# A hybrid attention and conv-FFN block: the first up-projection unit by token halves, pools moved in SBUF, two weight sums of the down-projection by DMA

## The chip, the cores and the metric

The kernel runs on one core of a Trainium2 chip. The metric is the device time of one execution in microseconds. Five engines are named as in the profile: PE (TensorE, with PEld for its weight loads), DVE (VectorE), ACT (ScalarE), POOL (GpSimd) and SP (SyncE, which here only issues DMAs).

## The reference

One residual block for 512 tokens of width 2048, in float32. The attention half has eight stick-breaking heads and eight latent-attention heads; it is not touched here. The rest is:

```python
mixed = concat(rmsnorm(o_sb), rmsnorm(o_mla))              # 512 x 2048
x = x + rmsnorm(mixed @ w_o, g_attn_post)
h = rmsnorm(x, g_ffn_pre)
u = causal_depthwise_conv(h @ w_up, conv_w, conv_b)        # w_up 2048 x 11264, width 3
gate, val = split(u, 2)                                    # 5632 columns each
y = (gelu(gate) * val) @ w_down                            # w_down 5632 x 2048
x = x + rmsnorm(y, g_ffn_post)
```

## The kernel before

**Arithmetic.** Each float32 operand is cut into a high part (a cast to a rounded type on ScalarE, `sc.copy`) and a low part (the difference, on VectorE). A product is three matmuls: high by high, high by low, low by high.

**Order of the work.** The program is straight-line. The framework gives each engine one list of instructions in order, which its planner makes at build time: it follows the program's order and pulls an instruction forward when, by its plan, its inputs and its page in SBUF are there. A tile of a pool takes a page that an older tile held and waits for that tile's last reader. Pools are stacked from the left or the right end of SBUF; a pool opened where another was closed waits page by page.

**The end of the out-projection** (lines 675 to 711 and 779 to 787). `w_o` is multiplied in column blocks; the last 512 columns go as two blocks of 256 (`sub`), each token tile of 128 rows at a time (`last_cols`). In the second block, each tile's rows are then complete: `residual(t)` (line 738) takes the row statistics (VectorE, then GpSimd for the power), adds x, squares on ScalarE, stores the new x by a DMA from GpSimd's queue, and scales the rows. `transposed(t)` (line 754) turns them by TensorE, multiplies by the gain in sixteen small ScalarE operations (line 763) and splits them into `act_hi` and `act_lo` (line 734). Order: columns of t, transposes of t - 1, residual of t.

**The up-projection** (lines 797 to 936). 22 units of 256 gate and 256 value columns. A unit is a 2 x 2 block product (inner halves of `w_up` by token halves and gate/value halves) done with seven products of half size in place of eight. The left operands of the seven are a11, a12, a7 (which takes the place of a21) and a22 in `act_hi`/`act_lo`, and the sums a5, a6, a3 in pages of their own; `transposed` makes them for t = 2 and 3. The weight side: four raw quarters of 1 MB are loaded per unit (buffers `wr`, 4), sums of them are formed in place by VectorE (`plus`, line 806), and each of the seven is cast and split (`w_parts`, lines 800 and 802; pages `wh` and `wl`, 3 each). Order p1, p5, p6, p7, p2, p3, p4. Weight parts are made two products ahead of their use (`queue`, line 1141). After a unit, the convolution and the gated product run in small steps between products (`later`), and the result goes to `g_dram`.

**The down-projection** (lines 939 to 1041). 20 of the 22 units in 5 chunks of 4, each chunk in two column halves `q`, each again a sevenfold product of 24 matmuls with 512 columns. At the start of a chunk (`q == 0`, product 1) `g_sides(ch)` loads the chunk's gated rows (`gr`, 2 MB) and makes all seven operand sides in the order g11, g22, g5, g6, g7, g12, g3. Each product is added to accumulators in SBUF (`add_to`, line 960; the first chunk copies on ScalarE). Before the first chunk `open_down` closes the pools of the up-projection and opens those of the down-projection. The last two units and the end of the block follow in `last_steps`.

## Time and profile before

| what | value |
|---|---|
| median of 3 runs (lowest, highest) | 2146.14 us (2144.24, 2147.12) |
| profiled execution: time, span | 2146.34 us, 2144.6 us |
| TensorE busy | 2037.9 us, 95% |
| VectorE busy | 1583.2 us, 74% |
| ScalarE busy | 944.1 us, 44% |
| GpSimd busy | 122.3 us, 6% |
| mean granted TensorE clock | 0.972 of full speed |

The page has the busy time by engine, the span in 40 slices, the DMA queues, the chain of work that ended last, and the costliest groups. Other views give the waits of an engine by what ended them, the instructions in order of time, and the busy time in chosen windows. A matmul's shown duration is longer than its distance to the next one, because matmuls are pipelined; rates are taken from windows with their counts. [...]

### The profile page before, as it was taken

Reading aid. Unit: us, or ns where it says so; the run is one execution under the profiler, and the core shown is the slowest. Engines: PE = TensorE matmul, PEld = TensorE weight load, DVE = VectorE, ACT = ScalarE, POOL = GpSimd, SP = SyncE. Lnnn points to the kernel's source line nnn. Section 1 sums busy time; section 2 is a strip of 40 time slices with the busy share of each in tenths; the row PEclk is TensorE's granted clock in tenths of the full one; section 3 lists DMA queues with packets and bytes.
Section 4 is the critical chain, followed back from the end, with each engine's and each line's share of the span. In section 5 each row is a group of like instructions: output and inputs, shape, how many; then the busy total and the mean of one; then the engine's idle time right before and its main releaser. Section 6 shows DMA issues by size and latency. Waiting matters only on the chain.

```text
span 2144.6 us, 30034 instructions
## 1 busy us (share of the span) xinstructions
PE 2037.9 (95%) x12784; PEld 1819.6 (85%) x12784; DVE 1583.2 (74%) x1491; ACT 944.1 (44%) x1124; POOL 122.3 (6%) x147
## 2 busy tenths in 40 slices
PE   8999999999999569999999999999997999999996
PEld 6788788877888569999999999999997778778785
DVE  7355355776233679989889889889889788999985
ACT  6243234455323854544444444444444543343332
POOL 0000001122021200000000000000000000000004
PEclk9999999999999779999999999999998999999998
DMA  8322322211422342342342432432434344324252
GB/s 273 98 71 77 98 76 63 76 33 60 143 93 79 118 150 96 110 156 90 126 140 89 139 127 89 155 111 96 155 105 147 128 138 138 118 79 160 96 175 99
DMA packets 179062, 245.16 MB, mean 114 GB/s; under 512 B 8176, under 2 KB 127088, under 8 KB 178928
## 3 DMA queue, kind: packets, MB, share of 16 engines
q1 hardware_dynamic: 174048, 227.04, 32.9%
q0 software_dynamic: 4448, 15.73, 1.8%
q8 instruction: 100, 1.64, 0.3%
q10 hardware_dynamic: 432, 0.47, 0.1%
q14 instruction: 34, 0.28, 0.0%
HBM read 223.29 MB, written 19.92 MB: 113 GB/s over the span
## 4 chain that ended last, share of the span: by engine, by line
PE 84%; DVE 8%; ACT 3%; DMA 2%; issue 1%; POOL 0%; DVEq 0%; ACTq 0%; POOLq 0%
PE ps L858 40%; PE ps L991 15%; PE ps L111 8%; PE ps L112 8%; PE ps L113 8%; PE ps L258 2%; DVE wr L806 1%; DVE wl L802 1%; DMA wr<-in_w_in_dram 1%; PE ps L234 1%; ACT wh L800 1%; DVE x L1094 1%; DVE t L438 1%; DVE wl L107 0%; ACT wh L105 0%
## 5 line engine op out<-in xcount | busy, mean ns | idle before, releaser
L800 ACT CAST wh<-wr 128x2048 fp32r<-128x2048 f32 x228 | 435.1, 1912 | 575.1 <-DVE wr L806 227.2
L802 DVE TENSOR_TENSOR wl<-wr,wh 128x2048 fp32r<-128x2048 f32 x228 | 519.1, 2288 | 111.5 <-ACT wh L800 111.1
L858 PE MATMUL ps<-act_hi,wh 128*128 128x256 f32 x1408 | 395.5, 281 | 15.0 <-ACT wh L800 15.0
L858 PE MATMUL ps<-act_hi,wl 128*128 128x256 f32 x1408 | 394.1, 280 | 1.5 <-DVE wl L802 1.5
L858 PE MATMUL ps<-act_lo,wh 128*128 128x256 f32 x1408 | 393.9, 280 | 0.0
L806 DVE TENSOR_TENSOR wr<-wr 128x2048 f32<-128x2048 f32 x128 | 292.6, 2286 | 1.3
L107 DVE TENSOR_TENSOR wl<-wr,wh 128x1024 fp32r<-128x1024 f32 (+2 forms) x105 | 128.1, 1220 | 210.4 <-ACT wh L105 210.3
L858 PEld LDWEIGHTS ps<-act_hi,wh 128*128 128x128 f32 x1408 | 265.5, 189 | 15.4 <-ACT wh L800 15.4
L858 PEld LDWEIGHTS ps<-act_hi,wl 128*128 128x128 f32 x1408 | 265.8, 189 | 1.8 <-DVE wl L802 1.8
L858 PEld LDWEIGHTS ps<-act_lo,wh 128*128 128x128 f32 x1408 | 264.5, 188 | 0.0
L105 ACT CAST wh<-wr 128x1024 fp32r<-128x1024 f32 (+2 forms) x105 | 108.0, 1028 | 234.3 <-PE ps L112 98.9
L111 PE MATMUL ps<-wh,act_hi 128*128 128x512 f32 (+1 forms) x448 | 163.9, 366 | 8.0 <-ACT act_hi L182 6.7
L112 PE MATMUL ps<-wl,act_hi 128*128 128x512 f32 (+1 forms) x448 | 163.3, 365 | 1.7 <-DVE wl L107 1.6
L113 PE MATMUL ps<-wh,act_lo 128*128 128x512 f32 (+1 forms) x448 | 162.9, 364 | 0.0
L111 PE MATMUL ps<-act_hi,wh 128*128 128x512 f32 x368 | 146.8, 399 | 0.0
L112 PE MATMUL ps<-act_lo,wh 128*128 128x512 f32 x368 | 145.7, 396 | 0.0
L113 PE MATMUL ps<-act_hi,wl 128*128 128x512 f32 x368 | 144.6, 393 | 0.0
L111 PEld LDWEIGHTS ps<-wh,act_hi 128*128 128x128 f32 x448 | 84.9, 190 | 22.6 <-ACT act_hi L182 6.7
L112 PEld LDWEIGHTS ps<-wl,act_hi 128*128 128x128 f32 x448 | 85.2, 190 | 16.9 <-DVE wl L107 2.4
L858 PE MATMUL ps<-a3h,wh 128*128 128x256 f32 x352 | 98.6, 280 | 0.0
L858 PE MATMUL ps<-a6h,wh 128*128 128x256 f32 x352 | 98.5, 280 | 0.0
L858 PE MATMUL ps<-a5h,wh 128*128 128x256 f32 x352 | 98.5, 280 | 0.0
(315 smaller groups left out, 4337.9 us busy)
## 6 DMA issues: line engine op xcount, KB each, us to landing
wr<-in_w_up_dram SPq DMA_DIRECT2D x88, 1024.0 KB, 5.4
wr<-in_w_down_dram SPq DMA_DIRECT2D x44, 1024.0 KB, 6.2
wr<-in_w_in_dram SPq DMA_DIRECT2D x59, 512.0 KB, 3.7
wr<-in_w_o_dram SPq DMA_DIRECT2D x32, 512.0 KB, 3.5
g_dram<-bg POOLq DMA_DIRECT2D x22, 512.0 KB, 5.2
gr<-g_dram SPq DMA_DIRECT2D x5, 2048.0 KB, 9.9
acc<-in_x_dram SPq DMA_DIRECT2D x16, 256.0 KB, 4.7
x<-in_x_dram SPq DMA_DIRECT2D x16, 256.0 KB, 5.4
```

Of the source, the lines that this page charges most:

```text
L105: sc.copy(hi, raw)
L107: ve.tensor_tensor(lo, raw, f(hi), ALU.subtract)
L111: te.matmul(ps, lh, rh, start=start, stop=False)
L112: te.matmul(ps, lh, rl, start=False, stop=False)
L113: te.matmul(ps, ll, rh, start=False, stop=stop)
L234: te.transpose(dst, a(b, j), ident)
L258: te.matmul(dst, q[:, b * P:(b + 1) * P], k[:, k0:S], start=i == 0, stop=False)
L800: sc.copy(hi, w)
L802: ve.tensor_tensor(lo, w, f(hi), ALU.subtract)
L806: ve.tensor_tensor(w, w, v, ALU.add)
L858: te.matmul(dst, l[:, k, ms], r[:, k, :], start=fresh and k == 0 and m == 0 and i == 0, stop=k == 7 and i == 2, skip_group_check=True)
L991: te.matmul(bs[t], l[:, k, ts_], r[:, k, :], start=fresh and k == 0 and i == 0, stop=k == FU - 1 and i == 2, skip_group_check=True)
```

## The change

1. The first up-projection unit is no longer a sevenfold product. Its gate part is done plainly, first for tokens 0 to 255 (needs only tiles 0 and 1 transposed), then, after the transposes of tiles 2 and 3, for tokens 256 to 511; its value part follows for all 512 tokens. Its gate weights are loaded and split before the last out-projection columns, into pages that later hold a5 and a6.
2. `transposed` runs two tiles behind the columns instead of one; the gain is one VectorE operation for 512 columns instead of four ScalarE operations; two of the four row scalings go to VectorE. The left sides a5, a6, a7, a3 are made in one go after the gate (`left_sides`). x rows and gains are loaded earlier, into fewer pages.
3. The pool of weight pages moves to the left end, where the later weight pool takes its place; the other pools move to the right. The down-projection's pages take the places of `act_hi`, `act_lo`, the a5, a6, a3 pages and small pages; nothing is closed in between.
4. In the down-projection the order is p1, p2, p5, p6, p7, p3, p4. The sums w12 + w22 and w11 + w21 are made by DMAs that add in flight (`accum_op`, issued by GpSimd), reading the quarters from HBM a second time; the other two stay on VectorE. The operand sides are made one by one: those of the next chunk each right after the product that used the old one in the second column half, those of the first chunk during and after the last up-projection unit, in halves of two units. Side 6 has pages of its own in the place of the unit's output pages.
5. Gated results are stored in two halves; the rows for the final residual come in four loads; some buffer counts and the DMA scratch size change.

The core of the diff (left out: unchanged helpers, page bookkeeping, the old bodies of functions that are replaced as a whole):

```diff
-    wp_stack, wp = stacked("wp", 4, "right")
+    wp_stack, wp = stacked("wp", 4)
...
-    at_stack, at = stacked("at")
+    at_stack, at = stacked("at", side="right")
...
-    cp_stack, cp = stacked("cp")
-    fp_stack, fp = stacked("fp")
+    cp_stack, cp = stacked("cp", side="right")
+    tp_stack, tp = stacked("tp", side="right")
+    fp_stack, fp = stacked("fp", side="right")
...
+    def load_x2(t):
+        for c in range(4):
+            x2[t, c] = fpage("x2", 8)
+            sy.dma_start(x2[t, c], x[t * P:(t + 1) * P, c * 512:(c + 1) * 512])
...
+            if c % 2:
+                ve.tensor_scalar_mul(y[t, c], x2[t, c], r2)
+            else:
+                sc.activation(y[t, c], x2[t, c], AF.Copy, scale=r2)
+        if t + 2 < NT:
+            load_x2(t + 2)
...
+            ve.tensor_tensor(raw[t, c].rearrange("p (k x) -> p k x", k=4), ps.rearrange("p (k x) -> p k x", k=4),
+                             g_rep[:, c, :, None].broadcast_to([P, 4, P]), ALU.mult)
+            split_into(((a11, a12), (a21, a22))[t // 2][c // 2], c, t, raw[t, c])
...
+    def left_sides():
+        a5, a6, a3 = ((cpage(n + "h"), cpage(n + "l")) for n in ("a5", "a6", "a3"))
+        for t in (2, 3):
+            for c in range(2):
+                x21, x22 = raw[t, c], raw[t, c + 2]
                 ve.tensor_tensor(x22, x21, x22, ALU.subtract)
-                split_into(a5, ks, th, x22)
+                split_into(a5, c, t, x22)
...
+    def gated(unit, m, bg, bv):
+        sc.activation(bg, bg, AF.Gelu_apprx_tanh)
+        ve.tensor_tensor(bg, bg, bv, ALU.mult)
+        po.dma_start(g_dram[unit, :, m, :], bg)
+    def early_w(kg):
+        raw_ = new_raw([P, 4, 256])
+        sy.dma_start(raw_, w_up[kg * 512:(kg + 1) * 512, 0:256].rearrange("(k p) c -> p k c", p=P))
+        both = cpage(("a5h", "a5l", "a6h", "a6l")[kg], (2, 4, 256))
+        hi, lo = both[:, 0], both[:, 1]
+        sc.copy(hi, raw_)
+        ve.tensor_tensor(lo, raw_, f(hi), ALU.subtract)
+        return hi, lo
...
+    def plain_part(banks, ws, kg, hs, first):
+        wh, wl = ws
+        for kk in range(4):
+            for m in range(2):
+                ms = slice(m * P, (m + 1) * P)
+                dst = banks[m][:, hs]
+                ah, al = act_hi[:, 4 * kg + kk, hs], act_lo[:, 4 * kg + kk, hs]
+                for i, (l, r) in enumerate(((wh, ah), (wh, al), (wl, ah))):
+                    te.matmul(dst, l[:, kk, ms], r, start=first and kg == 0 and kk == 0 and i == 0,
+                              stop=kg == 3 and kk == 3 and i == 2, skip_group_check=True)
+    load_x2(1)
     for sub in range(2):
         ws = [load_w(w_o, kg * 512, 4, 1536 + sub * 256, 256) for kg in range(4)]
+        if sub == 0:
+            ws_g = [early_w(kg) for kg in range(4)]
         for t in range(NT):
             last_cols(sub, ws, t)
             if sub == 1:
-                if t > 0:
-                    transposed(t - 1)
+                if t > 1:
+                    transposed(t - 2)
                 residual(t)
-    transposed(NT - 1)
+    bank_g = [bank(), bank()]
+    for kg in range(4):
+        plain_part(bank_g, ws_g[kg], kg, lo_half, True)
+        if kg == 1:
+            transposed(2)
+    ws_v = [load_w(w_up, kg * 512, 4, DFF, 256) for kg in range(4)]
+    transposed(3)
+    for kg in range(4):
+        plain_part(bank_g, ws_g[kg], kg, hi_half, False)
+    bank_v = [bank(), bank()]
+    for kg in range(4):
+        plain_part(bank_v, ws_v[kg], kg, slice(0, S), True)
+    pair_g, pair_v = (tp.tile([P, 2, S], F32, tag=n, name=n, bufs=1) for n in ("ug", "uv"))
+    for m in range(2):
+        conv(bank_g[m], m, pair_g[:, m])
+    a5, a6, a3 = left_sides()
+    def first_values(_):
+        for m in range(2):
+            conv(bank_v[m], NFF + m, pair_v[:, m])
+            gated(0, m, pair_g[:, m], pair_v[:, m])
     fp_stack.close()
-    vp_stack.close()
     wp_stack.close()
...
-    wq_stack, wq = stacked("wq", 1, "right")
-    tp_stack, tp = stacked("tp")
-    def w_parts(w):
-        n, cols = w.shape[1], w.shape[2]
-        hi = wq.tile([P, n, cols], R32, tag="wh", name="wh", bufs=3)
+    wq_stack, wq = stacked("wq")
...
         def p1():
-            w[11] = q(0, 0)
+            pair = w_pair(*shape)
+            w[11] = quarter(0, 0)
+            return w_parts(w[11], pair)
+        def p2():
+            w[21] = quarter(1, 0)
+            return w_parts(w[21])
+        def p5():
+            w[12] = quarter(0, 1)
+            plus(w[11], w[12])
+            if added:
+                added(w[12], 1, 1)
...
         def p6():
-            w[22] = q(1, 1)
-            return w_parts(plus(w[11], w[22]))
+            w[22] = quarter(1, 1)
+            parts = w_parts(plus(w[11], w[22]))
+            if added:
+                added(w[11], 1, 0)
+            return parts
         def p7():
-            return w_parts(plus(w[12], w[22]))
-        def p2():
-            w[21] = q(1, 0)
-            return w_parts(w[21])
+            return w_parts(w[12] if added else plus(w[12], w[22]))
         def p3():
             return w_parts(w[22])
         def p4():
-            return w_parts(plus(w[11], w[21]))
+            return w_parts(w[11] if added else plus(w[11], w[21]))
+        if added:
+            return p1, p2, p5, p6, p7, p3, p4
         return p1, p5, p6, p7, p2, p3, p4
...
         def half():
-            return tp.tile([P, 2, 256], F32, tag="u", name="u", bufs=3)
+            return v2(pg_v())
...
+            bg, bv = [pg_v() for _ in range(2)], z["bv"]
+            def last(m):
+                conv(ug[:, m], 2 * unit + m, bg[m])
+                gated(unit, m, bg[m], bv[m])
+            later.extend(lambda m=m: last(m) for m in range(2))
+        def then(use, *ns):
+            def both(w):
+                use(w)
+                if ns[0] == 6:
+                    open_down()
+                for n in ns:
+                    g_side(0, n)
+            return both
+        if unit == NFF // 2 - 1:
+            return zip(sevenfold(quarter, (8, 256)), (m1, m5, then(m6, 1), then(m7, 2), m2, then(m3, 5),
+                                            then(m4, 6, 7, 3, 4)))
+        return zip(sevenfold(quarter, (8, 256)), (m1, m5, m6, m7, m2, m3, m4))
...
+    def g_side(ch, n):
+        if n == 1:
+            gr = [cpage(tag, (2, 2, S), F32) for tag in ("a5h", "a5l")]
+            for i, t in enumerate(gr):
+                u0 = ch * FU + 2 * i
+                sy.dma_start(t, g_dram[u0:u0 + 2].rearrange("u p f s -> p u f s"))
+            d["gr"] = gr
+        def part(f_, h):
...
+        def added(w, kh, nh):
+            po.dma_start(w, rows(kh, nh), accum_op=ALU.add)
...
+        def use(n, w):
+            name = {1: "X", 2: "X", 5: "D", 3: "D", 7: "C", 4: "C", 6: "Y"}[n]
+            fresh = n in (1, 5, 7, 6)
+            if fresh:
+                z[name] = [bank(), bank()]
+            down_product(z[name], w, d["g"][n], fresh)
+            if q == 1 and ch + 1 < NST:
+                g_side(ch + 1, n)
...
     def stream():
-        for unit in range(NFF // 2):
+        yield (lambda: None), first_values
+        for unit in range(1, NFF // 2):
...
-    nc = bacc.Bacc("TRN2", target_bir_lowering=False, num_devices=1, dynamic_dma_scratch_size=1024)
+    nc = bacc.Bacc("TRN2", target_bir_lowering=False, num_devices=1, dynamic_dma_scratch_size=2048)
```

## Rows read from the trace of the kernel before

**Rows 1.** The page, part 1: busy us (share of the span) and instructions of each engine.

```profile
PE 2037.9 (95%) x12784; PEld 1819.6 (85%) x12784; DVE 1583.2 (74%) x1491; ACT 944.1 (44%) x1124; POOL 122.3 (6%) x147
```

**Rows 2.** Waits of TensorE, whole span: instruction, releaser, us in total, times, longest.

```profile
PE ps L759 <- ACT v L752: 24.0, 4, 13.4
...
PE ps L991 <- ACT g5h L964: 15.3, 4, 4.5
...
PE ps L858 <- ACT wh L800: 15.0, 1, 15.0
...
PE ps L991 <- ACT g11h L964: 12.7, 1, 12.7
```

**Rows 3.** Windows by stage: length, then PE, PEld, DVE, ACT, POOL busy, PEclk, DMA, GB/s.

```profile
640.00:680.00 40.00, 40.00 (x219) 34.34 (x218) 11.89 (x12) 12.54 (x21) 6.04 (x4) 1.00 0.26 87
...
700.00:772.00 72.00, 31.54 (x205) 29.28 (x203) 46.48 (x85) 57.83 (x153) 13.75 (x24) 0.68 0.41 140
...
814.00:1644.50 830.50, 830.50 (x7053) 830.45 (x7052) 718.50 (x526) 382.48 (x295) 11.27 (x21) 1.00 0.37 121
...
1644.50:1669.60 25.10, 9.35 (x31) 6.52 (x29) 23.24 (x22) 11.99 (x13) 0.53 (x1) 0.66 0.41 147
...
1836.50:1922.20 85.70, 81.23 (x336) 64.70 (x336) 79.21 (x62) 33.59 (x21) 0.00 (x0) 0.96 0.37 123
...
2083.00:2128.00 45.00, 44.88 (x193) 35.83 (x191) 25.60 (x33) 15.09 (x32) 19.72 (x15) 1.00 0.32 112
...
2128.00:2144.60 16.60, 0.00 (x0) 0.00 (x0) 9.42 (x14) 2.89 (x6) 5.59 (x5) 0.62 0.34 126
```

**Rows 4.** Timeline of ScalarE and TensorE: first evacuation of the last columns; eight transposes.

```profile
700.28 0.47 ACT L708 ACTIVATE y<-ps,rs 128x256 f32<-128x256 f32 x1 [2.91 <-PE ps L113]
...
708.90 1.97 PE L759 MATMUL ps<-ident,v 128*128 128x128 f32 x8 [4.12 <-ACT v L752]
```

**Rows 5.** Groups by line and form, VectorE: count, busy us and mean ns, idle before.

```profile
L107 DVE TENSOR_TENSOR wl<-wr,wh 128x1024 fp32r<-128x1024 f32 x95 | 119.1, 1254 | 207.3 <-ACT wh L105 207.2
...
L865 DVE SCALAR_TENSOR_TENSOR bg<-ug,gvc,bg 128x511 f32<-128x511 f32 x44 | 30.9, 745 | 0.0
...
L390 DVE TENSOR_SCALAR aT<-aT 128x512 f32<-128x512 f32 x4 | 1.7, 425 | 0.1
...
L734 DVE TENSOR_TENSOR a5l<-y,a5h 128x512 fp32r<-128x512 f32 x4 | 2.7, 684 | 0.0
...
L802 DVE TENSOR_TENSOR wl<-wr,wh 128x2048 fp32r<-128x2048 f32 x28 | 63.9, 2288 | 16.2 <-ACT wh L800 16.2
...
L965 DVE TENSOR_TENSOR g5l<-gr,g5h 128x1024 fp32r<-128x1024 f32 x5 | 6.1, 1217 | 0.0
```

**Rows 6.** Groups by line and form, ScalarE: weight casts and small gain copies.

```profile
L800 ACT CAST wh<-wr 128x2048 fp32r<-128x2048 f32 x228 | 435.1, 1912 | 575.1 <-DVE wr L806 227.2 <-PE ps L858 167.5 <-issue 108.1
...
L763 ACT ACTIVATE y<-ps,gv 128x128 f32<-128x128 f32 x32 | 10.0, 433 | 0.0
```

**Rows 7.** Timeline of VectorE, 690 to 790 us: first and thirteenth operation of a run.

```profile
759.84 0.69 DVE L734 TENSOR_TENSOR a5l<-y,a5h 128x512 fp32r<-128x512 f32 x1
...
767.06 0.68 DVE L734 TENSOR_TENSOR a6l<-v,a6h 128x512 fp32r<-128x512 f32 x1
```

**Rows 8.** Timeline of TensorE, 765 to 778 us: neighbouring matmuls of 256 columns.

```profile
773.08 0.41 PE L858 MATMUL ps<-act_hi,wh 128*128 128x256 f32 x1
...
773.29 0.41 PE L858 MATMUL ps<-act_lo,wh 128*128 128x256 f32 x1
```

**Rows 9.** DMA issues: queue, count, KB each, median us to landing.

```profile
wr<-in_w_down_dram SPq DMA_DIRECT2D x44, 1024.0 KB, 6.2
...
g_dram<-bg POOLq DMA_DIRECT2D x22, 512.0 KB, 5.2
...
gr<-g_dram SPq DMA_DIRECT2D x5, 2048.0 KB, 9.9
...
gl<-g_dram SPq DMA_DIRECT2D x2, 512.0 KB, 3.3
```

279 lines of the change are left out of this document (138 added, 141 removed).

## The prediction, before the change was run

> **What bounds the kernel now.** I read the page's totals first: TensorE is busy 95% of the span [rows 1]. So time can only come out of places where TensorE stands still or runs at its lower clock. Next the waits of TensorE, longest first [rows 2]: 24.0 us before transposes, 15.0 us before the first up-projection matmul, 12.7 us before the first down-projection matmul, 15.3 us in four waits for the operand g5. All lie in two places, which the stage windows show [rows 3]. From 700 to 772 us TensorE is busy 31.5 of 72 us at a mean granted clock of 0.68 of full speed. From 814 to 1644.5 it is busy all 830.5 us: 7053 matmuls, 0.1178 us each, 39.55 us for a unit of 336, so the up-projection proper has nothing to give. From 1644.5 to 1669.6 it is busy 9.4 of 25.1 us. A later chunk of the down-projection takes 85.7 us with VectorE busy 79.2 of them. The last stage, 2083 to 2128, gives the free rate of a 512-column matmul: 45.0 us for 193, 0.233 us.
>
> The profiled execution took 2146.34 us, its span 2144.6, 1.74 us around it; the median of the three runs is 2146.14. My sum is against 2146.34. About 0.2% (4.3 us) is what a measurement of this kernel can tell from no change.
>
> **Part A: the first unit by token halves.** Common point: the first tile of the last out-projection columns is evacuated at 700.28 us [rows 4]. What the change adds ahead of it are four gate-weight loads with their splits, beside matmuls, where from 640 to 680 us TensorE is never idle and VectorE is busy 11.9 of 40 [rows 3]; I cost them at nothing. Without that cover they would cost up to 4 x 1.25 us (line 107 of [rows 5]).
> Before: unit 1 starts at 814 us [rows 3].
> After, TensorE's work from 700.3 to unit 1: 144 matmuls of three token tiles x 0.1178 = 17.0; 64 transposes at 1.97/8 = 0.246 [rows 4] = 15.8; the plain unit has 192 gate matmuls of 256 columns x 0.1178 = 22.6 and 96 value matmuls of 512 x 0.233 = 22.4, together 45.0 (5.5 more than the 39.55 of the seven-product unit it replaces). Sum 77.8, so not before 778.
> After, VectorE's work from 702, by the groups of [rows 5]: for each token tile 4 residual adds at the 0.745 of line 865's like operation, 2 of the scalings that move from ScalarE at 0.425, 4 gain products (in place of sixteen small ScalarE copies, line 763 [rows 6]) and 4 low halves at 0.69, and for two evacuating operations of 256 columns with the tiny statistics another 2 x 0.69: 10.7, four tiles 42.8. Value weights 4 x 1.25 = 5.0. Gate convolution 4 x 0.745 = 3.0. The left operands, now in one piece after the gate, 32 operations at 0.60 (from the first to the thirteenth of such a run 7.2 us pass [rows 7]) = 19.3. First weight split of unit 1: 2.2. Sum 72.3, so not before 774 if it never idled. ScalarE, 57.8 of 72 us now [rows 3], sheds the 64 small copies, at most 27.7 us, and stops being the slowest there.
> The dependences add to this. Transposes of tile 3 are finished on VectorE at about 702 + 42.8 + 5.0 + 5 of idle in the statistics chains = 755. The upper gate half (11.3 us) has by then partly run at a lowered clock; I end it at 762. The left operands reuse the pages of the gate weights, so they start only then: 762 + 3.0 + 0.8 + 19.3 + 2.2 = 787.3; the value product, 22.4 us, ends at 784 and hides most of it. Unit 1 starts at about 788: gain 814 - 788 = 26 us. Bounds: 36 if everything fits (778). At the other end the plain unit runs half at the lower clock, where a 256-column matmul takes 0.21 us [rows 8], which adds about 10, and the first raw weight waits for pages that the left operands hold, which adds a load of 6.2 [rows 9] and a cast and a low half of 1.9 + 2.3 [rows 5, 6]: some 20 in all, unit 1 at 808, gain 6. Putting the weight pool low bears on that last point alone: the conversion pages of the new pool then lie over the old weight pages, and the diff doesn't show which raw buffer lies over which late page.
>
> **Part B: the down-projection.** TensorE's work after the up-projection is 1680 + 192 matmuls x 0.2332 = 436.5 us; it took 2128 - 1644.5 = 483.5 [rows 3]. So 47 us are lost, 32.8 of them named waits (12.7 + 15.3 [rows 2] and two smaller ones), the rest the low clock after them.
> Why they are there: the seven operand sides of a chunk are made in one piece at its start. The g22 pages are held by the last product of the old chunk, and g5 is made after g22. The change makes each side right after its last use in the second half of the old chunk, and puts product 4 last: six products (6 x 5.6 us) of lead. The four waits for g5 go. Late next would be a weight of the next group: its raw buffer is freed by the split of product 4, as now, three products (16.8 us) ahead of its use, and load, cast and low half take 6.2 + 4.2. The loads of the gated rows, now two of 1 MB, stand among the weight loads on SP's queue and would hold those up if their pages were not free; the pages are last read for side 4 of the old chunk, seven products earlier.
> VectorE for a chunk: 79.2 us [rows 3], minus 4 sums by DMA x 2.29 (the size of line 802 [rows 5]) = 9.2, plus about 1.5 because 11 side operations of 1.217 [rows 5] become 22 of 0.684: 71.5, under TensorE's 336 x 0.2332 = 78.4. VectorE stops being the slower one.
> First chunk: sides 1, 2 and 5 are made during the last unit. Behind it VectorE has the last convolutions (3.0), gate products (1.4), side 6 (2.5; its page lies over the unit's output pages, so it waits for the convolution) and weight operations for products 5 and 6 (9.1): about 17 us against three products (16.8 us) before side 6 is needed. I leave 5 us there, 1 us at each of 4 chunk ends, 2 us of clock: loss 11 instead of 47, gain 36. Bounds: 46 if nothing stalls, 20 if VectorE still sets half of the waits.
>
> **The accumulating DMA** is not in the trace. Below, 6.2 us, a plain load of 1 MB; 9.9 us, 2 MB in one transfer; above, 19.8, twice that, if the destination is read and written again as separate passes [rows 9]. GpSimd's queue issues it; a 512 KB store from there lands after 5.2 us, a load of that size from SP after 3.3 [rows 9]. I take 10. How late may it be? For product 7 the sum into w12 can start when product 1 starts, and its split (1.9 + 2.3 us) must end when product 6 ends: 4 x 5.6 - 4.2 = 18 us. Below that it costs nothing; each microsecond above costs one in each of 10 groups. 19.8 would cost 18 us. Queued behind it on GpSimd is only the other sum, needed two products later; but VectorE and ScalarE take their queues in order, so a late sum also holds the PSUM additions behind it.
> [...]
>
> Edits with one answer: pool sides, tags, fewer spare buffers for statistics and junk, x rows and gains loaded earlier, the gated pages stored in halves (two issues on an idle queue), the final x2 rows as four larger loads. Each lies beside matmuls; zero. The tail after the last matmul (16.6 us) is unchanged.
>
> **Sum.** 2146.34 - 26 - 36 = 2084.3.
>
> **Rivals.** (1) Part A stalls elsewhere: VectorE's queue and the lowered clock eat it. For it: VectorE and TensorE have nearly equal sums (72 and 78) with crossing dependences, and the clock in the same stretch is 0.68 now. Against: ScalarE sheds up to 27.7 us. Gain 6: 2146.3 - 6 - 36 = 2104.
> (2) VectorE remains the bound of the down-projection, or the sums come at the upper bound. Against: the margin is 7 us a chunk. Gain 20 or 36 - 18: 2146.3 - 26 - 19 = 2101.
> (3) The sums by DMA are late: slower. If one takes L us, the loss is 10 x (L - 18) us; the 62 us are gone at L = 24.2, and at L = 30 the time is 2084 + 120 = 2204. [...] Against: it would have to be 14 us above the value taken, and the stores from that queue, issued while VectorE was 87% busy [rows 3], land 1.9 us later than a load from SP [rows 9]; hence its low chance.
> [...]
> (4) The planner places the sides or the new unit where they were: only one part works, 2110 to 2120.
>
> **How the numbers follow.** Forecast 0.68 (2062 to 2100), rival 1 0.11, rival 2 0.08, rival 4 with less than 0.2% left 0.03 and otherwise 0.03, rival 3 0.07. Predicted 2084. Low end: both best bounds, 2146 - 36 - 46 = 2064, less 2 for the transposes' clock: 2062. High end: both worst, 2146 - 6 - 20 = 2120. Outside is about 0.12. Faster by over 0.2%: 0.90; within: 0.03; slower: 0.07.
>
> **What would show it.** In the waits of TensorE, the lines on transposes and on g5 gone or below 3 us each; the first matmul of the second unit at 778 to 808; a chunk of 336 matmuls in 79 to 80 us; VectorE some 72 us in it. The issue list shows 20 accumulating transfers of 1 MB from GpSimd with their landing time: over 18 us, and a wait of TensorE or VectorE at product 7 must appear. Wrong would be a new wait before the left operands of the second unit longer than 10 us, or a granted clock under 0.8 in the plain unit.

## The result and the profile after

The changed kernel takes 2087.59 us (median of 4 runs, 2084.47 to 2090.9) against 2145.19 for the kernel before in the same comparison; the ratio is 0.9731, with a 95% interval of 0.9714 to 0.9748. The forecast was 2084.3, with a range of 2062 to 2120.

The profiled execution took 2090.9 us, its span 2089.1. Engine totals of the changed kernel (beside [rows 1]), and the longest waits of TensorE (beside [rows 2]: engine, tile, line, waited for, total, times, longest):

```profile
PE 2028.6 (97%) x12736; PEld 1821.4 (87%) x12736; DVE 1537.8 (74%) x1570; ACT 924.4 (44%) x1114; POOL 162.6 (8%) x189
```

```profile
PE ps L836 <- ACT act_hi L748: 9.9, 2, 7.5
PE ps L111 <- ACT act_hi L182: 7.8, 1, 7.8
PE ps L133 <- DVE diag L132: 6.4, 3, 5.4
PE ps L1117 <- DVE wl L884: 4.6, 3, 3.0
PE ps L1117 <- DVE act_hi L1055: 3.6, 4, 1.0
PE ps L945 <- DVE wl L884: 3.2, 1, 3.2
PE ps L945 <- ACT wh L883: 2.7, 1, 2.7
```

The 24 us before the transposes, the 12.7 us at the first down-projection matmul and the four waits for an operand side are gone. New is 9.9 us in the plain unit (L836). Line 945 is the up-projection's product, 1117 the down-projection's; line 884 makes a weight's low half, line 1055 adds a product from PSUM, where TensorE leaves it, to its accumulator in SBUF.

Stage windows of the changed kernel (window, length, busy us and instruction count of TensorE, weight loads, VectorE, ScalarE, GpSimd, then granted clock as a share of full speed, DMA share, GB/s), beside [rows 3]; the row from 784.20 to 789.20 is the start of the second unit, the two from 1626.40 on are the start of the down-projection:

```profile
560.00:640.00 80.00, 80.00 (x354) 66.23 (x354) 25.50 (x24) 23.87 (x35) 13.08 (x9) 1.00 0.42 136
...
700.00:772.00 72.00, 61.89 (x429) 57.88 (x429) 62.98 (x115) 43.84 (x90) 14.60 (x23) 0.93 0.38 131
...
784.20:789.20 5.00, 4.97 (x23) 4.98 (x24) 4.96 (x3) 1.90 (x1) 0.00 (x0) 0.50 0.03 12
784.20:1605.00 820.80, 820.77 (x6874) 820.78 (x6875) 702.94 (x526) 373.84 (x305) 21.17 (x39) 1.00 0.36 118
860.00:900.00 40.00, 40.00 (x338) 40.00 (x337) 34.29 (x27) 18.26 (x15) 1.08 (x2) 1.00 0.37 119
...
1626.40:1642.40 16.00, 12.21 (x53) 9.23 (x51) 15.96 (x23) 10.90 (x17) 1.10 (x2) 1.00 0.72 188
1642.40:1646.40 4.00, 3.98 (x11) 3.12 (x11) 2.89 (x2) 1.68 (x1) 0.00 (x0) 0.57 1.02 421
...
1860.00:1940.00 80.00, 79.04 (x342) 63.73 (x341) 71.54 (x71) 34.14 (x29) 5.15 (x4) 1.00 0.71 188
```

From 700 to 772 us TensorE is busy 61.9 of 72 us at a clock of 0.93, where it was busy 31.5 at 0.68. A chunk's 336 matmuls take 79 to 80 us (the same matmul of three chunks starts at 1794.86, 1874.60 and 1953.70), where one took 85.7. VectorE is busy for about 71 of 80 us there. At the start of the down-projection TensorE is busy for 12.2 of 16 us, and then at a clock of 0.57 for 4.

The two spans, cut at the same events (first evacuation of the last out-projection columns; start of steady work on the second unit; end of the up-projection; last matmul; end):

| stretch | before, us | after, us | difference | forecast |
|---|---|---|---|---|
| to the first evacuation | 700.3 | 695.9 | -4.4 | 0 |
| to the second unit | 113.7 | 88.3 | -25.4 | -26 |
| 21 units of the up-projection | 830.4 | 842.2 | +11.8 | 0 |
| down-projection and last stage | 483.1 | 445.6 | -37.5 | -36 |
| tail | 17.1 | 17.1 | 0 | 0 |
| span | 2144.6 | 2089.1 | -55.5 | -62 |

The two terms of the sum came out as forecast. Two stretches that I had costed at nothing moved by -4.4 and +11.8 us, and they are the whole 7 us by which this execution is above the forecast. The experiments ask whether the two terms are right for the reasons given, and where the other two come from.

### The profile page after: what moved, and what is told of

Read it like the earlier page. It is cut to its first block, busy times and chain, and to the rows that moved or that the text cites. A ratio compares the mean times of both kernels' runs of the same rounds, so it can differ in the third digit from the quotient of the medians.

```text
span 2089.1 us, 30179 instructions
## 1 busy us (share of the span) xinstructions
PE 2028.6 (97%) x12736; PEld 1821.4 (87%) x12736; DVE 1537.8 (74%) x1570; ACT 924.4 (44%) x1114; POOL 162.6 (8%) x189
## 4 chain that ended last, share of the span: by engine, by line
PE 81%; DVE 10%; DMA 4%; ACT 3%; issue 2%; POOL 0%; DVEq 0%; ACTq 0%; SPq 0%; POOLq 0%
PE ps L945 38%; PE ps L1117 12%; PE ps L111 9%; PE ps L112 9%; PE ps L113 9%; PE ps L258 2%; DVE wl L884 2%; PE ps L836 2%; DMA wr<-in_w_in_dram 1%; PE ps L234 1%; DMA wr<-in_w_down_dram 1%; DVE wr L888 1%; ACT wh L883 1%; DMA a5l<-g_dram 1%; DVE t L438 1%
## 5 line engine op out<-in xcount | busy, mean ns | idle before, releaser
L883 ACT CAST wh<-wr 128x2048 fp32r<-128x2048 f32 x221 | 421.7, 1912 | 606.5 <-DVE wr L888 275.0
L884 DVE TENSOR_TENSOR wl<-wr,wh 128x2048 fp32r<-128x2048 f32 x221 | 505.4, 2288 | 152.0 <-ACT wh L883 151.9
L945 PE MATMUL ps<-act_hi,wl 128*128 128x256 f32 x1344 | 381.7, 284 | 3.2 <-DVE wl L884 3.2
L945 PE MATMUL ps<-act_hi,wh 128*128 128x256 f32 x1344 | 381.5, 284 | 2.7 <-ACT wh L883 2.7
L945 PE MATMUL ps<-act_lo,wh 128*128 128x256 f32 x1344 | 381.2, 284 | 0.0
L945 PEld LDWEIGHTS ps<-act_hi,wl 128*128 128x128 f32 x1344 | 258.8, 193 | 3.4 <-DVE wl L884 3.4
L888 DVE TENSOR_TENSOR wr<-wr 128x2048 f32<-128x2048 f32 x104 | 237.8, 2287 | 1.2
L113 PE MATMUL ps<-wh,act_lo 128*128 128x512 f32 (+1 forms) x512 | 186.3, 364 | 0.0
L113 PEld LDWEIGHTS ps<-wh,act_lo 128*128 128x128 f32 x512 | 97.1, 190 | 15.7 <-DVE act_lo L183 0.4
L1117 PE MATMUL ps<-wh,act_lo 128*128 128x512 f32 x320 | 100.3, 390 | 0.0
```

Source lines behind the costliest of these rows:

```text
L113: te.matmul(ps, ll, rh, start=False, stop=stop)
L883: sc.copy(hi, w)
L884: ve.tensor_tensor(lo, w, f(hi), ALU.subtract)
L888: ve.tensor_tensor(w, w, v, ALU.add)
L945: te.matmul(dst, l[:, k, ms], r[:, k, :], start=fresh and k == 0 and m == 0 and i == 0, stop=k == 7 and i == 2, skip_group_check=True)
L1117: te.matmul(bs[t], l[:, k, ts_], r[:, k, :], start=fresh and k == 0 and i == 0, stop=k == FU - 1 and i == 2, skip_group_check=True)
```

## Experiments: the two parts

**The first unit as seven products again.** Edit: the plain unit and its early weights are taken out, the stream starts at unit 0.

```
-        yield (lambda: None), first_values
-        for unit in range(1, NFF // 2):
+        for unit in range(NFF // 2):
```

> The changed kernel with the first up-projection unit as seven products again, all else of the change kept (transposes evacuated by one VectorE operation, rows loaded early, sides of the pools, down-projection). Theory: the unit by token halves is what covers the transposes and the left operands; without it unit 2 starts some 25 us later and the time is 2109 to 2114. Rival: the evacuation of the transposes on VectorE and the unloaded ScalarE brought half of it or more; then 2095 to 2103.

Measured: 2111.63 us (2110.32 to 2113.1), 24.0 above the changed kernel. The theory held. Its waits and the same window:

```profile
PE ps L925 <- ACT wh L863: 25.0, 2, 24.9
PE ps L775 <- ACT v L767: 15.0, 2, 7.7
```

```profile
700.00:772.00 72.00, 29.52 (x202) 28.06 (x201) 64.65 (x106) 38.55 (x74) 11.18 (x18) 0.72 0.39 133
```

TensorE is back at 29.5 of 72 us although VectorE evacuates the transposes and ScalarE is unloaded (38.6 us, 57.8 before). From the first evacuation to the second unit's steady work it takes 112.6 us, against 113.7 before: these edits gave about 1 us by themselves. What gave the 24 us is work for TensorE that needs only what is ready.

**The two weight sums on VectorE again.**

```
-            if added:
-                added(w[12], 1, 1)
...
-            return w_parts(w[12] if added else plus(w[12], w[22]))
+            return w_parts(plus(w[12], w[22]))
```

(and the same for the sum into w[11].)

> The changed kernel with the two weight sums of products 7 and 4 on VectorE again (order 1, 2, 5, 6, 7, 3, 4 and everything else kept). Theory: the sums by DMA are worth what VectorE is then over TensorE's time. VectorE for a chunk goes from 71.5 to 71.5 + 4 x 2.29 = 80.7 us against TensorE's 78.4 to 79, so a chunk of 336 matmuls takes about 81 us instead of 79.5 and the whole 2093 to 2103 us, with the changed kernel at 2087.6. Rival: most of the gain of the down-projection hangs on the sums; a chunk goes back to the 85.7 us of before and the time to about 2087.6 + 5 x 6 = 2118. Second rival: the margin lies elsewhere and nothing changes, 2085 to 2090.

Measured: 2095.64 us (2094.03 to 2099.6), +8. One window of it:

```profile
1860.00:1940.00 80.00, 77.05 (x333) 61.92 (x332) 77.61 (x71) 33.12 (x28) 0.00 (x0) 1.00 0.39 129
```

333 matmuls in 80 us make about 81 us a chunk (the same matmul of the next chunk starts 81.3 us later), with VectorE busy 78. The theory held, and the sums by DMA are worth 8 us of the 37.5.

**The sides in one piece at the chunk's start.**

```
-            if q == 1 and ch + 1 < NST:
-                g_side(ch + 1, n)
+            if n == 1 and q == 0 and ch > 0:
+                for m in ORDER:
+                    g_side(ch, m)
```

> The changed kernel with the seven operand sides of the next chunk made in one piece at that chunk's start, as the kernel before does, instead of one after each product of the old chunk's second half (the sums by DMA stay). Theory: the lead of six products removed the four waits for sides; without it they come back at the four chunk starts, 3.8 us each as in the kernel before, with some 1.2 us of others each: 2087.6 + 20 = about 2108, and the waits of TensorE show sides at four places. Rival: with VectorE no longer the slower engine it makes the sides in time wherever they stand in the program: below 2093.

Measured: 2082.54 us (2079.66 to 2086.8), ratio 0.9697 (0.968 to 0.9713): no slower, and if anything 5 us faster. The theory fell. No wait for a side came back; TensorE's two longest waits in the down-projection (the second was 3.6 us in the changed kernel):

```profile
PE ps L1117 <- DVE wl L884: 4.1, 2, 3.0
PE ps L1117 <- DVE act_hi L1055: 1.2, 2, 0.7
```

**Both undone at once.** The edits of the last two together.

> The changed kernel with both undone at once: the two sums on VectorE and the seven sides made in one piece at each chunk's start; the order of products with 4 last, the pages of the sides and the sides made in the last up-projection unit stay. Each alone cost 8 us or nothing. Theory: either suffices to keep VectorE ahead, and both undone bring the waits at four chunk starts back, 5 us each on top of the 8: 2087.6 + 8 + 20 = about 2115. Rival: the order of the products and the separate pages of the sides did it, since no side then waits for the last product of the old chunk but the one that is needed last; then no more than the sums alone, 2093 to 2099.

Measured: 2094.72 us (2094.42 to 2096.19), the same as with only the sums undone. So the rival held: the six products of lead were not what removed the waits, with the sums by DMA or without. What this kernel still has of part B is the new order and the first chunk's sides in the last up-projection unit. Product 4 was last before too, and every side had pages of its own. New in the order is that product 2 stands between 1 and 5, and that side 4 (g22 before), whose page the old chunk's last product holds, is made last and not second. The sums carry 8 us of the 37.5, and the distance between matmuls, which other starts of the operands changed (below), about 4.5. So the order and the first chunk's sides carry some 25 us. How they share them was not tried.

The trace of the kernel before shows why TensorE waited for g5. One chunk start:

```profile
1826.27 1.06 ACT L964 CAST g22h<-gr 128x1024 fp32r<-128x1024 f32 x1 [0.45 <-PE ps L991]
...
1833.37 1.22 DVE L974 TENSOR_TENSOR gr<-gr 128x1024 f32<-128x1024 f32 x1
...
1831.83 3.70 ACT L800 CAST wh<-wr 128x2048 fp32r<-128x2048 f32 x2 [4.50 <-DVE wr L806]
1835.43 1.04 ACT L964 CAST g5h<-gr 128x1024 fp32r<-128x1024 f32 x1
...
1836.53 0.80 PE L991 MATMUL ps<-wh,g5h 128*128 128x512 f32 x1 [4.46 <-ACT g5h L964]
```

Side g22 starts when the old chunk's last product releases its page (0.45 us of idle, ended by TensorE). The difference for g5 is formed in place on VectorE, after g22 is done there, and its cast stands behind two weight casts on ScalarE. Where side 4 is made last, g5 no longer stands behind it, whether the sides are made early or late. That fits the run above, but no run goes back to the old order alone.

## Experiments: how late a sum by DMA may be

The landing time was the value taken. From the changed kernel's list of DMA issues (KB each, median us from issue to landing):

```profile
wr<-in_w_down_dram SPq DMA_DIRECT2D x44, 1024.0 KB, 7.0
...
wr<-in_w_down_dram POOLq DMA_DIRECT2D x20, 1024.0 KB, 10.0
```

Then each sum was lengthened by repeating it:

```
-            po.dma_start(w, rows(kh, nh), accum_op=ALU.add)
+            for _ in range(2):
+                po.dma_start(w, rows(kh, nh), accum_op=ALU.add)
```

> The changed kernel with each accumulating transfer made twice, the second behind the first into the same tile (so its output isn't the reference's): a sum then takes 20 us instead of 10. Theory (the threshold of the prediction): the sum for product 7 has 18 us, so 2 us are lost in each of 10 groups: 2087.6 + 20 = about 2108. Rival: the sum for product 4, issued behind product 6's split, has less; in the trace of the changed kernel it is issued at 1726 us and its cast and low half are done at 1740.8, some 4 us ahead of its product, so the threshold is 14 us, 6 us are lost in each group, and the time is about 2148.

> The changed kernel with each accumulating transfer made three times, one behind the other into the same tile (so its output isn't the reference's): a sum then takes 30 us. Theory (10 x (L - 18) us): 2087.6 + 120 = about 2208. Rival (threshold of 14 us, by the sum for product 4): 2087.6 + 160 = about 2248. If the sums are hidden by more than either says, below 2150.

Measured: 2245.04 us with two (+157, 15.7 for each of ten groups) and 2404.19 with three (+317). Both theory (+20, +120) and rival (+60, +160) were far too low. To see which sum it is, only that for product 7 was repeated:

```
                 added(w[12], 1, 1)
+                added(w[12], 1, 1)
```

> The changed kernel with only the sum for product 7 made twice, the second behind the first into the same tile, 20 us instead of 10 (so its output isn't the reference's); the sum for product 4 once. Both twice cost 157 us where the threshold of 18 us gave 20. Theory: the sum for product 7 has its 18 to 20 us (in the trace of the changed kernel it is issued at 1747.15 us and its cast must start by 1767.3), and the loss came from the sum for product 4: 2088 to 2108. Rival: a late cast of product 7 holds back everything behind it on ScalarE and VectorE, the splits for the next group and with them its own next sum among them, so that the loss comes round in each group: about half of the 157, 2165.

Measured: 2138.41 us (2135.71 to 2139.58), +51, where the free time of 18 to 20 us allowed at most 20; the rival (2165) was too high. The rows show how it goes. First and last issue of these transfers in the four kernels, from the line's own view (changed kernel; one sum twice; both twice; both thrice):

```profile
L1134 POOL DMA_DIRECT2D wr<-in_w_down_dram x20: 1268/1286/1368, 1623.8 to 2003.3; - x20
```

```profile
L1135 POOL DMA_DIRECT2D wr<-in_w_down_dram x30: 1283/1294/1369, 1619.3 to 2050.1; - x30
```

```profile
L1135 POOL DMA_DIRECT2D wr<-in_w_down_dram x40: 1282/1293/1367, 1619.9 to 2159.4; - x40
```

```profile
L1135 POOL DMA_DIRECT2D wr<-in_w_down_dram x60: 1275/1286/1371, 1621.0 to 2320.4; - x60
```

Ten groups stretch over 379.5, 430.8, 539.5 and 699.3 us: ten transfers more cost 51, the next ten 109, the next twenty 160. That is 5.1, 10.9 and 8.0 us for each transfer that is added to a group. So the transfers of a group are paid one after the other, those of the one sum and those of the other. GpSimd's and ScalarE's timelines of the kernel with one sum twice show a group (start, duration, then what ended the idle time before):

```profile
1709.99 1.28 POOL L1135 DMA_DIRECT2D wr<-in_w_down_dram  x1 [20.63 <-DVE act_lo L1086]
1720.26 1.29 POOL L1135 DMA_DIRECT2D wr<-in_w_down_dram  x1 [8.99 <-DMA wr<-in_w_down_dram]
1734.47 1.28 POOL L1135 DMA_DIRECT2D wr<-in_w_down_dram  x1 [12.92 <-issue]
1754.66 1.29 POOL L1135 DMA_DIRECT2D wr<-in_w_down_dram  x1 [18.91 <-DVE act_hi L1056]
```

```profile
1734.26 1.90 ACT L883 CAST wh<-wr 128x2048 fp32r<-128x2048 f32 x1 [12.33 <-DMA wr<-in_w_down_dram]
...
1743.38 1.92 ACT L883 CAST wh<-wr 128x2048 fp32r<-128x2048 f32 x1 [3.34 <-DMA wr<-in_w_down_dram]
```

ScalarE stands 12.3 us at the cast that waits for the sum of product 7; the sum for product 4 leaves GpSimd only at 1734.47, when that cast has begun; its own cast holds ScalarE again; and the next group's first sum leaves at 1754.66, 20 us behind. The casts of the next group's weights stand behind both. So the time to compare with TensorE's group (39 to 40 us) is not one sum's lead but the way round: both sums one behind the other and some 12 to 15 us of casts, low halves and VectorE additions. With 20 and 10 us a group takes 5.1 us more than the changed kernel's 39.5, which is 30 + 14.6; with 20 and 20 it takes 16.0 more, 40 + 15.5; with 30 and 30 32.0 more, 60 + 11.5. With 10 and 10 it would be 32 to 36: the changed kernel has 4 to 8 us in hand for both sums together, an estimate from these rows. What held the second sum until then the profile doesn't name ("issue"). The program makes it wait only for its loads and for the low half of product 6, which VectorE ended at 1727.4, 7 us earlier. But it leaves 0.3 us after the transfer ahead of it on GpSimd's queue has landed (1734.16), and in six of the ten groups of this run the profile names nothing for that wait (53.6 us of "issue" in all). In the changed kernel the second sum leaves 0.32 to 0.34 us after that landing in four of the ten groups, and none of its 20 sums leaves before the one ahead has landed. So these sums did not overlap here; why is open.

## Experiments: where operands start

**What costs 12 us in the up-projection.** Nothing in it waits (820.77 of 820.80 us busy), yet 40 us hold 338 matmuls (row 860 to 900 above) where they held 342. The first 5 us of it are at a clock of 0.50, behind the wait before the second unit: 24 matmuls start where 42 would, which makes about 2 of the 12. For the rest: in the trace the distance from one matmul to the next is 0.1200 us for products on act_hi and act_lo and 0.1178 for those on a5, a6 and a3; before it is 0.1178 for all. In the out-projection the reverse: 354 matmuls in 80 us (row 560 to 640 above), 349 before. The same two windows of the kernel before:

```profile
560.00:640.00 80.00, 80.00 (x349) 64.63 (x348) 24.64 (x23) 22.44 (x34) 13.12 (x9) 1.00 0.39 135
860.00:900.00 40.00, 40.00 (x342) 40.00 (x341) 34.66 (x27) 18.56 (x16) 0.53 (x1) 1.00 0.36 119
```

Two kernels of little but matmuls measured this by itself.

> Not the computation of the reference: only matmuls on float32r operands whose places in SBUF are set by hand, 96 of 256 columns (or 48 of 512) for each pair of places, first with the other engines nearly idle, then with VectorE, ScalarE or a load into SBUF working beside them near to and far from the operands. It is to tell why the spacing of 256-column matmuls in the changed kernel is 0.1200 us where weights and moving operand both lie low in SBUF and 0.1178 where they lie apart. Theory: the place alone decides, so the quiet stages show two levels, about 0.120 where both operands lie close together at one end and 0.118 where they lie apart. Rival: accesses of other engines collide with TensorE's reads; then all quiet stages are alike, and only the stages with traffic near the operands are longer, by some 0.002 us a matmul.

Stages of 256 columns and of 512 columns with the other engines nearly idle, then 256 columns beside VectorE, ScalarE and loads:

```profile
40.00:240.00 200.00, 200.00 (x1669) 200.00 (x1668) 11.92 (x18) 0.00 (x0) 0.00 (x0) 1.00 0.00 1
290.00:490.00 200.00, 200.00 (x884) 165.61 (x883) 24.90 (x36) 0.00 (x0) 0.00 (x0) 1.00 0.00 1
500.00:570.00 70.00, 70.00 (x586) 70.00 (x585) 50.49 (x27) 7.31 (x4) 0.00 (x0) 1.00 0.00 1
572.00:640.00 68.00, 68.00 (x569) 68.00 (x568) 4.30 (x7) 36.52 (x20) 0.00 (x0) 1.00 0.08 23
642.00:710.00 68.00, 68.00 (x569) 68.00 (x569) 4.71 (x11) 0.00 (x0) 0.00 (x0) 1.00 0.90 325
```

Both theories fell: 0.1200 us (0.2267 for 512 columns) at every place, and with all the traffic tried, near or far, a load at 325 GB/s among it: from copy to copy 96 matmuls take 11.47 to 11.58 us in every stage of 256 columns, 11.52 in most, beside VectorE, ScalarE and loads alike. All operands here start at the same offset modulo 256 bytes, which the kernels' do not, and that gave the next kernel:

> Not the computation of the reference: matmuls on float32r operands only, with nothing beside them, 48 of 256 columns (then 24 of 512) for each of 59 pairs of starting bytes of the weights and of the moving operand, counted past a multiple of 512. The run on places showed one spacing for every place and for traffic of any kind: 0.1200 us for 256 columns, 0.2267 for 512, all with both operands on the same multiple of 128 bytes. In the two kernels a pair with 0.1200 (or 0.2267) has both operands at the same offset modulo 128 bytes, a pair with 0.1178 (or 0.2333) at offsets that differ by 64. Theory: the offset of the one operand against the other modulo 128 decides; a pair (0, 64) or (64, 0) gives 0.1178 and 0.2333, a pair (64, 64) 0.1200 and 0.2267. Rival: the start of the moving operand alone decides, then (0, 64) and (64, 64) are alike; or the start has no effect and all pairs are at 0.1200, so that something else of the kernels makes it.

A matmul here has two operands: the weights, 128x128, each behind a weight load (12736 loads and 12736 matmuls in the changed kernel), and the moving operand of 256 or 512 columns (in the out- and down-projection the weights of a matmul are the activations' side). Of 59 pairs of starting bytes those with both at multiples of 64 bytes fall into four cases by their difference (moving minus weights, modulo 256; distance between matmuls in us):

| difference | 256 columns | 512 columns |
|---|---|---|
| 0 | 0.1200 | 0.2267 |
| 64 | 0.1178 | 0.2289 |
| 128 | 0.1187 | 0.2333 |
| 192 | 0.1133 | 0.2333 |

Each stage of 48 matmuls ends with a copy by VectorE, so the distance between two copies is the length of a stage. The stages with weights at 64 and the moving operand at 0, 64, 128 and 192 end at 109.06, 120.48, 131.80 and 137.50:

```profile
103.61 0.69 DVE L80 COPY res<-ps 128x512 f32<-128x512 f32 x1 [4.98 <-PE ps L78]
109.06 0.69 DVE L80 COPY res<-ps 128x512 f32<-128x512 f32 x1 [4.75 <-PE ps L78]
114.73 0.69 DVE L80 COPY res<-ps 128x512 f32<-128x512 f32 x1 [4.98 <-PE ps L78]
120.48 0.69 DVE L80 COPY res<-ps 128x512 f32<-128x512 f32 x1 [5.06 <-PE ps L78]
126.14 0.69 DVE L80 COPY res<-ps 128x512 f32<-128x512 f32 x1 [4.97 <-PE ps L78]
131.80 0.69 DVE L80 COPY res<-ps 128x512 f32<-128x512 f32 x1 [4.96 <-PE ps L78]
137.50 0.69 DVE L80 COPY res<-ps 128x512 f32<-128x512 f32 x1 [5.00 <-PE ps L78]
```

They take 5.45 us (difference 192), 5.75 (0), 5.66 (64) and 5.70 (128). The stages up to 58 us, with weights at 0 and 256 columns, are about 2% shorter at each difference (5.64 us at 0, 5.53 at 64, 5.59 at 128, 5.33 at 192) and are not in the table; no run shows why.

The theory held in its kind (the difference decides), with four levels modulo 256 instead of two modulo 128. It is not the difference alone: pairs off the multiples of 64 lie between 0.1133 and 0.1233 us (48 matmuls in 5.44 to 5.92 us). The operands of both kernels start 32 bytes past a multiple of 64. (The starts are those of the built programs; no trace has them.) Four pairs of this kind were measured: a difference of 0 gave 0.1200 and 0.2267 us, 64 gave 0.1178 and 0.2289, 192 gave 0.1178 and 0.2333. So for these operands the table holds but for 192 with 256 columns, which in these two kernels only short stages have.

In the kernel before, the up-projection is all at a difference of 64 (0.1178), the out- and down-projection at 192 (0.2333). In the changed one act_hi and act_lo against the weights are at 0 (0.1200), a5, a6 and a3 at 64 (0.1178); the out-projection is at 0 (0.2267), the down-projection at 192 for five sides (0.2333) and at 0 for the two in act_lo (0.2267). These are the distances found in the two traces. 4032 of the 7056 matmuls of the 21 units by 0.0022 us make 9 of the 11.8 us lost, and the low clock behind the wait the other 2.

**The kernel with other starts.** Only padding: 224 bytes fewer of small buffers below the operands, 32 bytes at the top, 64 ahead of the weight pool, so that the up-projection is at 192 throughout and the down-projection at 64. The 32 bytes bring the operands to multiples of 64; without them the difference of 192 would have given 0.1178 by the pairs measured.

```
+    po.memset(pad.tile([P, 8], F32, name="pad"), 0.0)
...
+    po.memset(wq.tile([P, 16], F32, name="wpad"), 0.0)
```

> The changed kernel with nothing but the starting bytes of its operands moved: 224 bytes fewer below the operands on the left side, 32 bytes at the top of the right side, 64 bytes ahead of the up- and down-projection's weights, so that in the up-projection every moving operand starts 64 bytes before its weights modulo 256, both at multiples of 64. By the run on starting bytes a 256-column matmul then takes 0.1133 us in place of 0.1200 (four of seven products) and 0.1178 (three of seven), and the down-projection's 512-column matmuls 0.2289 in place of 0.2333 (five of seven) and 0.2267 (two). Theory: the spacing carries over to the kernel: a unit of 336 takes 38.1 us instead of 40.0, 21 units 800 instead of 842, the down-projection some 4 us less; 2087.6 - 42 - 4 = about 2042. Rival: VectorE and ScalarE, 34 us of a unit, with their queue order become late and eat half: about 2065. Second rival: the spacing in the kernel has another cause and nothing changes: 2085 to 2090.

Measured: 2053.83 us (2049.49 to 2079.03), ratio 0.9563 (0.9547 to 0.9579): 34 us faster than the changed kernel, between theory and rival. One of the five executions, the profiled one, took 2079.03, the others, of which there is no trace, 2049.5 to 2054.5. In it 8 us hold 73 matmuls at first; behind one wait, at 793 us, 40 us hold 342 to the end of the up-projection, which is 0.1178 again:

```profile
784.00:792.00 8.00, 8.00 (x73) 8.00 (x72) 5.99 (x4) 3.65 (x4) 0.00 (x0) 1.00 0.00 0
800.00:840.00 40.00, 40.00 (x342) 40.00 (x341) 33.03 (x25) 18.27 (x15) 0.54 (x1) 1.00 0.30 95
```

So in one execution the spacing of 0.1133 was lost at a wait, where 0.64 us pass from one matmul to the next. The last kernel below waits at the same matmul, which there starts 0.43 us after the one before it, and keeps 0.1133. What switches it stays open.

## Experiments: a version that beats both

The changed kernel waits before its second unit. VectorE's timeline there:

```profile
768.88 0.69 DVE L749 TENSOR_TENSOR act_lo<-v,act_hi 128x512 fp32r<-128x512 f32 x1
778.03 1.43 DVE L810 SCALAR_TENSOR_TENSOR uv<-ps,gvc,uv 128x511 f32<-128x511 f32 x2 [8.46 <-ACT uv L809]
...
781.89 2.28 DVE L884 TENSOR_TENSOR wl<-wr,wh 128x2048 fp32r<-128x2048 f32 x1
```

The left operands end at 769.6; the next instruction in the queue is the value convolution, which needs the end of the value product; the weight split stands behind it, and TensorE waits for the split.

```
+        cast, low = made[2]
+        with tc.issue_after(cast), tc.issue_after(low):
```

> The changed kernel with the value convolution and gated product of the first unit queued on ScalarE and VectorE behind the weight splits of the second unit's first three products, instead of ahead of them. Theory: VectorE stands idle from 769.6 to 778.0 us because its next instruction waits for the end of the value product, and the first weight split stands behind it; with the split in that gap the second unit starts at about 778 instead of 784, which gives 5 to 6 us: 2082. Rival: the split waits anyway, since the pages of the new weights lie over those of the value weights, which the value product reads to its end; then at most 2 us: 2086.

Measured: 2080.89 us (2079.05 to 2081.29), 6.7 below the changed kernel. The theory held: the low half is made at 768.35 and the second unit starts at 773.5 us without a wait. That the raw weight's page, and not the queue, held it is refuted.

All three (this one behind the fourth split, the starts, the sides at the chunk's start):

> The changed kernel with three edits together: the starting bytes of the operands as in e7_starts (alone 2053.8 us, against 2087.6), the first unit's value convolution and gated product queued behind the weight splits of the second unit's first four products (behind three it alone gave 2080.9), and the sides made at each chunk's start (alone 2082.5). Theory: the first two add up, the third gives 0 to 5 us: 2053.8 - 6.7 - 2.5 = about 2045, between 2041 and 2050. In the profiled execution of e7_starts the spacing changed from 0.113 to 0.118 us at one wait of TensorE of 0.6 us at 793 us and stayed there to the end of the up-projection, and this execution took 2079 us, 25 more than the other four; the convolution behind the fourth split takes away the wait in that place, so the rival is in the profile alone: with the spacing held at 0.113 its up-projection lasts 800 us, else 832.

Measured: 2042.59 us (2041.15 to 2043.21, 5 runs), ratio to the kernel before 0.9515 (0.9502 to 0.9528): 45 us faster than the changed kernel. Here the profiled execution kept the spacing through the whole up-projection, 7011 matmuls in 795 us:

```profile
785.00:1580.00 795.00, 794.83 (x7011) 794.43 (x7010) 715.10 (x549) 386.33 (x320) 22.84 (x42) 1.00 0.39 129
```

## Why the prediction was right, and where it was not

**Part A, the mechanism: right, and shown. The size: right in part by luck.** Gain 25.4 us in the profiled execution, 24.0 by the kernel that undoes it, 26 forecast; the 2 us at low clock behind the wait at 784, which the table books under the up-projection, take it to about 23. Single steps differ. The plain unit ran at a clock of 0.93, where I had given some of it the low one, and tile 3 and the gate's upper half ended earlier than I had them (51.6 and 60.3 us behind the common point, against 54.7 and 61.7). The left operands were done 73.7 us behind it, not 84.8: the planner put the first of them ahead of the gate convolution. But the first weight split stood in VectorE's queue behind the value convolution, which I had not placed at all and which needs the end of the value product: 8.5 us idle, of which the later kernel got 6.7 back. The total came out right because the two errors cancel, and that is luck. My lower bound was too mild as well: half of the plain unit's 45.0 us at 0.21 in place of 0.1178 us adds some 17.6 us, not 10. The rule to keep: of each engine, write down the order of the queue up to the instruction that the next stage needs, not the sum of its work alone.

**Part B, the size: right, 4 us of it by luck; the reason: half wrong.** 37.5 us against 36, the loss 13.3 against 11: 445.6 less 432.3, with 1200 matmuls at 0.2333 and 672 at 0.2267. So the stalls that went make 33.3 us, and 4 us came from the starts, a term that I had put at nothing. "VectorE stops being the slower one" is shown, with 71 of 80 us as worked out, and worth 8 us. "Six products of lead" is refuted: without the lead there is no loss. Nor did the change put product 4 last, as I wrote: it was last before. My other half, that side 5 stood behind a page that the old chunk's last product held, is what the trace of the kernel before shows, and it fits the kernels that make side 4 last; but no run isolates it. The 5 us that I left at the first chunk's start did occur, though not for the side that I named. The last up-projection matmul starts at 1626.4 us and the first of the down-projection at 1626.5, but in the 16 us from there TensorE stands still for 3.8, 3.0 of them for the low half of a weight on VectorE, and then runs 4 us at a clock of 0.57. "About 17 us" of VectorE's work there was added wrongly: its four terms make 16.0, under the 16.8 available.

**The accumulating DMA, its duration: right; its margin: wrong.** I took 10 us and 10.0 was measured; in this kernel that is 1.4 times a plain load of 7.0. The step "each microsecond above 18 costs one in each of 10 groups" failed. It priced each sum by itself against the time to its product, and did not follow a group round: both sums, one behind the other, come before the next group's first sum through ScalarE's queue. At the upper bound of 19.8 us I charged 18 us; two sums of 20 cost 157. So by an estimate from these runs rival 3 was decided not at 24.2 us but between 14 (a straight line from 0 at 10 us to 157 at 20) and 17 (6.2 us a group beyond 8 in hand), inside my own bounds of 6.2 to 19.8; no run has a sum between 10 and 20 us. The change was closer to a loss than my 0.07 says, and my high end of 2120 did not cover what it claimed to cover.

**"Zero" for the pools' sides: wrong twice.** I wrote that the low weight pool bears on the first raw weight alone. It moved the starts of nearly all operands against each other. In the up-projection that cost 9 of the 11.8 us. Ahead of the common point, where 4.4 us were gained, the table gives 6.4 for 960 matmuls of 512 columns that went from 192 to 0 (576 of them in the out-projection) and 2.4 for 1104 of earlier projections that went from 64 to 0; two waits there are 3.1 us longer than before (7.8 and 6.4 us, 6.7 and 4.4 before). Within part B it gives 4.5 (480 matmuls of two sides and 192 of the last stage, 0.0067 us each). The price stood in the trace as one number, 0.1178 us a matmul, that I took for a constant of TensorE.

## What to carry to other kernels

When a transfer joins a loop, don't compare its duration with the time to its use; add up the way round from its issue to its next issue, with every in-order queue on it, and compare that with the loop's period. Fill the time in which a chain of small steps runs with work on what is already there, and then look at what stands ahead of the next stage's first instruction in each queue. Treat moving a buffer as a change of TensorE's rate (0.1133 to 0.1200 us for a matmul of 256 columns here) until the spacing of its matmuls has been looked at.

## What the runs showed of the hardware

- The distance between float32r matmuls depends on where weights and moving operand start against each other modulo 256 bytes: 0.1133 to 0.1200 us for 256 columns and 0.2267 to 0.2333 for 512, both at multiples of 64 bytes and at a granted clock of 1.00, behind the first 58 us of the run on starting bytes. The best difference isn't the same for the two widths. With both operands 32 bytes past a multiple of 64 a difference of 192 gave 0.1178 instead of 0.1133 for 256 columns; other pairs lie between 0.1133 and 0.1233.
- At a difference of 0 it did not depend on the places tried within SBUF, nor on what VectorE, ScalarE or loads did there: 0.1200 us beside each of them, 11.47 to 11.58 us for 96 matmuls. GpSimd was not tried.
- At a difference of 192 two spacings occurred in one execution, 0.1133 and from a wait of TensorE on 0.1178; in the profiled execution of the last kernel 0.1133 lasted through a wait at the same matmul.
- An accumulating transfer of 1 MB from HBM into SBUF took 10.0 us (median of 20; 8.7 to 13.4), a plain load of that size beside it 7.0, with VectorE busy 89% of the time.
- Accumulating transfers of 1 MB from GpSimd's queue did not overlap: repeated into the same tile, the next waited for the landing of the one before (95.3 us in ten waits) and left 9.8 to 13.2 us behind its issue in the four groups from 1709 to 1858 us (the run with one sum twice). A sum into another tile, too, left only when the one ahead had landed, 0.32 us behind it or more (the changed kernel).
